# Hybrid decoder trunk: attention by pairs of tiles, and linear attention's scores of two chunks in one stretch

## The chip, the cores and the metric

The kernel runs on one core of a Trainium2 chip. The metric is the device time of one execution in microseconds (us); the time of a kernel is the median over its runs. An engine's busy time in the profile is the time in which it has at least one instruction in flight. The five engines are TensorE (PE, with its weight loads shown apart as PEld), VectorE (DVE), ScalarE (ACT), GpSimd (POOL) and SyncE (SP), which here issues most of the transfers.

## The reference

Two layers over a sequence of 1024 tokens with 1024 features, all in float32. A layer normalises the tokens, modulates them by a conditioning vector, projects them to the inputs of three groups of heads, gates the three outputs and projects them back:

```python
h = rms_norm(x, pre_gain) * (1.0 + scale) + shift
aq, ak, av, ag, rq, rk, rv, rg, gq, gk, gv, gg, ga = jnp.split(h @ w_in, IN_SPLITS, axis=-1)
a_out = sliding_window_attention(rot(aq), rot(ak), av, sinks) * silu(ag)      # 8 heads, 2 for keys and values
r_out = rms_norm(retention(rot(rq), rot(rk), rv)) * silu(rg)                  # 4 heads, chunks of 128
log_a = log_sigmoid(ga @ gla_gate_w + gla_gate_b) / 16
g_out = rms_norm(gated_linear_attention(gq, gk, gv, log_a), gain) * silu(gg)  # 4 heads, decay per key channel
x = x + gate * rms_norm(concat(a_out, r_out, g_out) @ w_out, post_gain)
```

Sliding-window attention looks back 128 tokens: a tile of 128 queries sees its own tile (keys up to the query) and the tile before it (keys after the query's place). A learned sink takes part in each softmax. Gated linear attention goes by chunks with a state that is carried from chunk to chunk:

```python
sc = einsum('bhid,bhijd,bhjd->bhij', qi, decay, ki)            # decay between i and j, per key channel
out = einsum('bhij,bhjv->bhiv', sc, vi) + einsum('bhid,bhdv->bhiv', qi * exp(b), state)
state = exp(b_last) * state + einsum('bhjd,bhjv->bhdv', ki * exp(b_last - b), vi)
```

## The kernel before

The 1024 tokens are eight tiles of 128 (t), in two halves of four (hf). A big projection is a sum of 24 matmuls over the full 128 by 128 array into one PSUM buffer of the pool `mm` (three buffers): each operand is split into a high and a low part, and three of the four products are summed. These matmuls are the stream that fills TensorE. Everything else on TensorE (scores, values, transposes, states) writes buffers of the pool `aux`, which has the other five of the eight PSUM banks, used in turn.

The order of TensorE's program is made by a small planner when the kernel is built. `clk` counts the estimated TensorE time of what is issued so far. Work beside the big projections is written as generators (`job`); a `yield` gives an estimated latency, from the table `L`, and may name a flag that must be set first; `pump`, called after every few matmuls of the stream, lets each job that is due issue its next step. So `L` doesn't delay anything on the chip: it says how far behind one step the next is placed in TensorE's program. Where a result is late on the chip, TensorE waits at that place, since its program is in order; so do the other engines, whose programs are in the order in which the jobs issue.

In a layer the order is gates, retention's inputs, linear attention's inputs, keys and values, queries of attention with their rotation (`attn_rot`, four times), attention's gates (`gate`, eight times), and the output projection (`y_half`). The small work is placed between these.

*Attention.* `attn_run` goes through the halves, the two groups of four heads (g) and the tiles, 16 (t, g) in a layer. For each, `attn_q` issues at once: the scores, 12 matmuls that use half of the array's rows each (64 features of a head; two of them run side by side), into two buffers of `aux`; the copy of the earlier tile's scores by ScalarE (`sprev`, L145) into the tile `smx`, and over it a masked copy of the own tile's scores by VectorE (L790); the maximum (L792), four exponentials on ScalarE (L795), a reciprocal (L798) and the normalisation on GpSimd (L799). The latency aq3 later it transposes the four heads' weights into one `aux` buffer (L176, `smx`), ScalarE copies them (`pf0`), GpSimd masks a second copy (L810). The latency aq4 later come the values: with the earlier tile's values `va` for all weights, and with the difference `vd` of own and earlier values for the masked ones: two matmuls each, in two passes (four in the trace), that use half of the array's columns. ScalarE copies the result (`aoc`), and a transfer puts it into `aoS` in DRAM, from where `gate` takes it when all four tiles of a half are there; the gated result goes to `mixS`, and the output projection loads it. Three `smx` tiles are in use in turn (SMB), and `load_mix` of the first two tiles waits for the flags ("s", l, 1, g) that attn_q sets when it issues the last scores of a half.

*Linear attention.* `gla_core` treats two chunk tiles (c) of 128 tokens as a pair p. For each c its scores are 28 matmuls of 32 columns, in two passes each (56 in the trace), that use a quarter of the array's rows, in four `aux` buffers, one for a head; ScalarE and VectorE bring them to `scz` (L985, L986). Then, the latencies gc3 and gc4 later, for each c: the part from the state (`stG`), the part from the scores, and, but for the last tile, the chunk's own addition to the state: four matmuls, in two passes, that use a quarter of the array's columns each (L1005), into a further `aux` buffer, which VectorE adds to `stC`.

Of the kernel before, what the change touches and what calls it, by code (L numbers as in the profile page):

```python
# [17 lines left out]
P = 128  # L18
# [71 lines left out]
def trunk(ctx: ExitStack, tc: tile.TileContext, ins, cst, out):  # L90
# [14 lines left out]
    def nm(s):  # L105
        uid[0] += 1
        return f"{s}_{uid[0]}"
# [75 lines left out]
    def job(gen):  # L183
        jobs.append([clk[0], None, gen])
# [579 lines left out]
    def attn_q(l, t, g, q):  # L764

        sm = gp.tile([P, 4, 129], F32, tag="smx", name=nm("smx"), bufs=SMB)
        V.tensor_copy(sm[:, :, 128], sink8[:, l, 4 * g:4 * g + 4])
        if t == 0:
            G.memset(sm[:, :, 0:128], -1e30)
        else:  # L770
            vd = gp.tile([P, P], F32, tag="vd", name=nm("vd"), bufs=3)
            G.tensor_tensor(vd, kv["v"][t], kv["v"][t - 1], ALU.subtract)
        pss = [aux(), aux()]
# [9 lines left out]
        if t % 4 == 3:  # L783
            flag(("s", l, t // 4, g))
        for r in range(2):
            pv = pss[r][:, 0:2 * n].rearrange("p (j c n) -> p j c n", j=2, n=P)
            sv = sm[:, r:4:2, 0:128]
            if t > 0:
                copy("sprev", sv, pv[:, :, 0, :])
            V.copy_predicated(sv, curmask.unsqueeze(1).to_broadcast((P, 2, P)), pv[:, :, n // P - 1, :])  # L790
        mx = small(4)
        V.tensor_reduce(mx, sm, AX.X, ALU.max, negate=True)  # L792
        sums = small(4)
        for h in range(4):
            A.activation(sm[:, h, :], sm[:, h, :], AF.Exp, bias=mx[:, h:h + 1],  # L795
                         accum_out=sums[:, h:h + 1])
        rs = small(4)
        V.reciprocal(rs, sums)  # L798
        eng("pn").tensor_tensor(sm[:, :, 0:128], sm[:, :, 0:128], rs.unsqueeze(2).to_broadcast((P, 4, P)), ALU.mult)  # L799
        yield lat("aq3", l)  # L800

        pp = aux()
        for h in range(4):
            transp(pp[:, h * P:(h + 1) * P], sm[:, h, 0:128], ident)
        pf = t2()
        copy("pf0", pf, pp)
        parts = [(kv["v"][max(t - 1, 0)], pf)]
        if t > 0:
            pr = t2()
            G.affine_select(h4(pr), h4(pf), [[0, 4], [1, P]], ALU.is_ge, 0.0, base=0, channel_multiplier=-1)  # L810
            parts.append((vd, pr))
        yield lat("aq4", l)
        po = aux()
        for q, (vt, pvv) in enumerate(parts):
            for r in range(2):
                mult(po[64 * r:64 * r + 64, 0:256].rearrange("p (j n) -> p j n", j=2), vt[:, 64 * r:64 * r + 64],
                     h4(pvv)[:, r:4:2, :], q == 0, q == len(parts) - 1, 0.215)
# [125 lines left out]
    def gla_core(l, p, qk, vs):  # L943
# [26 lines left out]
        A.activation(kbn, pt[:, 0:256], AF.Copy)  # L970
        for c in range(2):
            sp = [aux() for _ in range(4)]
            for s in range(1, 4):
                for h in range(4):
                    r = slice(32 * h, 32 * h + 32)
                    mult(sp[h][:, P + 32 * s:P + 32 * s + 32], kxz[r, s - 1, c],
                         q1[r, P * c + 32 * s:P * c + 32 * s + 32], True, True, 0.054)
            for s in range(4):
                for h in range(4):
                    r = slice(32 * h, 32 * h + 32)  # L980
                    dst = sp[h][:, 0:P].rearrange("p (b i) -> p b i", i=32)[:, :, 8 * s:8 * s + 8]
                    mult(dst, kds[s][r, P * c:P * c + P], cb32(ad[:, 0:256])[r, c, :, 8 * s:8 * s + 8],
                         True, True, 0.054)
            for h in range(4):
                A.activation(scz[:, c, h, 32:P], sp[h][:, P + 32:2 * P], AF.Copy)  # L985
                V.copy_predicated(scz[:, c, h, :], mask2, sp[h][:, 0:P])  # L986
            yield lat("gc3", l)
        yield lat("gc4", l)
        for c in range(2):
# [12 lines left out]
            if t < NT - 1:  # L1002
                pst = aux()
                for h in range(4):
# [314 lines left out]
L = {"tt1": 6.37, "tt2": 5.54, "tb1": 24.5, "tb2": 0.75, "pf3": 13.2, "pf1": 7.06, "pf2": 4.16, "mod1": 5.11, "mod2": 4.0, "mod3": 15.1, "mod4": 7.04, "mod5": 3.36, "mod6": 5.14, "pre1": 7.44, "kv1": 3.1, "kv2": 2.11, "aq1": 4.8, "aq7": 6.0, "ag1": 5.44, "aq2": 2.4, "aq6": 6.0, "aq3": 10.9, "aq4": 6.32, "aq5": 1.14, "hn1": 8.12, "hn2": 2.85, "gz1": 10.06, "gz2": 14.05, "gl1": 4.6, "gd3": 15.9, "gc1": 0.62, "gc2": 1.95, "gc3": 1.33, "gc4": 1.41, "gc6": 0.22, "gc5": 1.04, "rc1": 0.8, "rc2": 1.09, "rc3": 2.38, "rc4": 2.79, "fin1": 11.25, "lay1": 0.9, "mod2@1": 4.0, "mod3@1": 15.1, "mod5@1": 3.36, "mod6@1": 5.14, "pre1@1": 7.44, "kv1@1": 3.1, "kv2@1": 2.11, "aq1@1": 4.8, "aq7@1": 6.0, "ag1@1": 6.38, "aq2@1": 2.4, "aq6@1": 6.0, "aq3@1": 10.9, "aq4@1": 6.32, "aq5@1": 1.14, "hn1@1": 8.12, "hn2@1": 2.85, "gz1@1": 10.06, "gz2@1": 14.05, "gl1@1": 4.6, "gd3@1": 15.9, "gc1@1": 0.62, "gc2@1": 1.95, "gc3@1": 1.33, "gc4@1": 0.58, "gc6@1": 0.22, "gc5@1": 1.04, "rc1@1": 0.8, "rc2@1": 1.09, "rc3@1": 2.38, "rc4@1": 2.79, "fin1@1": 11.25, "lay1@1": 0.9}  # L1319
CHUNK = 7  # L1320
VDB = 8
FIN = 1
# [31 lines left out]
```

## Time and profile before

| | |
|---|---|
| time, median of 3 runs | 1030.42 us (1029.62 to 1031.78) |
| profiled execution: its time | 1029.6 us |
| its span | 1029.6 us |
| TensorE busy | 986.5 us, 96% |
| VectorE busy | 657.0 us, 64% |
| ScalarE busy | 385.2 us, 37% |
| GpSimd busy | 283.4 us, 28% |

A row of the timeline has the start, the length from the first start to the last end, the engine, line and operation, the tiles written and read (`out<-in`), the rows and columns of the array in use (64*128: half of the rows), the shape of the moving operand, and how many instructions the row merges. Matmuls overlap, so the length of a row reaches into the next; the time that a stretch takes is read from its start to the next row's start. In windows, a row has the stretch, its length, and the busy time of PE, PEld, DVE, ACT and POOL with the number of instructions; with a tile's name it has those engines alone that touch that tile. `arena` and `mx` hold weights and tokens of the big projections; but in rows with `kT,mx` the tile is the queries, and in `t,mx 32*128` linear attention's keys.

### The profile page before, as it was taken

How to read it: one execution, taken by the hardware profiler on the slowest of the kernel's cores; microseconds unless marked ns; L12 is line 12 of the kernel's file. 1: busy time of each engine (PE TensorE's matmuls, PEld its weight loads, DVE VectorE, ACT ScalarE, POOL GpSimd, SP SyncE). 2: the span in 40 equal slices, each digit the busy share in tenths (PEclk: the TensorE clock that was granted, in tenths of full speed). 3: DMA queues.
4: the chain of work that ended last, by engine and by line, in shares of the span. 5: the costliest groups of instructions: out<-in, count | busy, mean ns of one | idle time of the engine just before them, and what ended most of it. 6: DMA issues, size and time to landing. Idle time of an engine off the chain costs nothing.

```text
span 1029.6 us, 19500 instructions
## 1 busy us (share of the span) xinstructions
PE 986.5 (96%) x7185; PEld 837.6 (81%) x7185; DVE 657.0 (64%) x1597; ACT 385.2 (37%) x1098; POOL 283.4 (28%) x310
## 2 busy tenths in 40 slices
PE   5799999899999999999998999989999999999997
PEld 1588899888898777778888999988899877777886
DVE  3789856857657786664587395686676476653322
ACT  2465421323222565532353332123332266552111
POOL 2333101424231345421243120133233134532000
PEclk8899999999999999999998999999999999999999
DMA  9741613523326244687545151234132323445753
GB/s 324 270 133 52 180 50 103 147 84 101 99 78 195 76 147 129 213 264 224 189 146 162 42 164 53 79 111 124 34 107 73 113 82 98 149 123 184 226 190 137
DMA packets 124412, 140.47 MB, mean 136 GB/s; under 512 B 12718, under 2 KB 95640, under 8 KB 124316
## 3 DMA queue, kind: packets, MB, share of 16 engines
q1 hardware_dynamic: 116316, 127.50, 40.2%
q10 hardware_dynamic: 8000, 11.72, 3.2%
q8 instruction: 57, 0.93, 0.4%
q14 instruction: 39, 0.32, 0.1%
HBM read 102.48 MB, written 34.60 MB: 133 GB/s over the span
## 4 chain that ended last, share of the span: by engine, by line
PE 75%; DVE 11%; issue 3%; DMA 2%; POOL 2%; ACT 1%; SPq 0%; DVEq 0%; POOLq 0%; ACTq 0%
PE mm L161 58%; PE aux L161 13%; PE aux L176 4%; DVE arena L478 2%; DMA st<-in_w_mod_dram 1%; POOL sm L514 1%; DVE t L573 1%; DMA mx<-mixS 1%; DVE acc L361 1%; DVE t L420 0%; DVE t L544 0%; DVE t L844 0%; DVE t L1022 0%; DVE arena L147 0%; DVE t L924 0%
## 5 line engine op out<-in xcount | busy, mean ns | idle before, releaser
L161 PE MATMUL mm<-arena,arena 128*128 128x256 f32 (+2 forms) x1824 | 302.5, 320 | 6.0 <-DVE t L1092 3.8
L161 PE MATMUL mm<-arena 128*128 128x256 f32 (+2 forms) x1824 | 300.5, 318 | 7.2 <-ACT arena L577 3.0
L161 PEld LDWEIGHTS mm<-arena,arena 128*128 128x128 f32 x1824 | 256.0, 191 | 31.9 <-issue 4.0
L161 PEld LDWEIGHTS mm<-arena 128*128 128x128 f32 x1824 | 255.2, 191 | 31.3 <-issue 5.1
L161 PE MATMUL mm<-arena,mx 128*128 128x512 f32 (+1 forms) x816 | 184.9, 385 | 0.5 <-DMA mx<-mixS 0.5
L161 PEld LDWEIGHTS mm<-arena,mx 128*128 128x128 f32 x816 | 145.7, 188 | 34.7 <-issue 1.9
L514 POOL TENSOR_TENSOR sm<-sm,mhalf 128x1 f32<-128x1 f32 (+1 forms) x64 | 54.0, 845 | 329.2 <-DVE sm L513 318.5
L478 POOL TENSOR_TENSOR arena<-st,arena 128x512 fp32r<-128x512 f32 x66 | 95.7, 1459 | 104.6 <-ACT arena L145 75.3
L145 ACT ACTIVATE t<-aux 128x256 f32<-128x256 f32 (+2 forms) x112 | 52.5, 473 | 105.2 <-PE aux L176 62.0
L799 POOL TENSOR_TENSOR smx<-smx,sm 128x512 f32<-128x512 f32 x32 | 36.2, 1131 | 127.3 <-DVE sm L798 108.0
L478 DVE TENSOR_TENSOR arena<-st,arena 128x512 fp32r<-128x512 f32 x62 | 64.9, 1055 | 4.3 <-PE mm L161 2.7
L795 ACT ACTIVATE smx<-smx,sm 128x129 f32<-128x129 f32 x128 | 49.9, 392 | 34.5 <-DVE sm L792 29.1
L145 ACT ACTIVATE arena<-st 128x512 fp32r<-128x512 f32 x90 | 53.1, 625 | 21.3 <-PE mm L161 14.8
L361 DVE SCALAR_TENSOR_TENSOR acc<-st,c_act,acc 128x512 f32<-128x512 f32 x60 | 48.7, 812 | 17.3 <-DMA st<-in_w_mod_dram 17.0
L176 PE MATMUL aux<-c_ident,t 128*128 128x128 f32 x288 | 47.4, 282 | 7.7 <-DVE t L544 5.4
L1077 ACT ACTIVATE t<-mm 128x512 f32<-128x512 f32 x30 | 17.9, 596 | 97.0 <-PE mm L161 45.7
L1078 DVE TENSOR_TENSOR t<-mm,modg 128x512 f32<-128x512 f32 x30 | 20.7, 689 | 44.5 <-ACT t L1077 44.5
L1113 DVE SCALAR_TENSOR_TENSOR t<-t,sm,t 128x512 f32<-128x512 f32 x32 | 25.2, 813 | 35.9 <-DMA t<-xs 20.5
L176 PEld LDWEIGHTS aux<-c_ident,t 128*128 128x128 f32 x288 | 34.2, 143 | 13.9 <-DVE t L544 6.9
L161 PEld LDWEIGHTS aux<-t,mx 32*128 32x128 f32 (+1 forms) x896 | 40.1, 187 | 5.1 <-issue 3.2
L838 ACT ACTIVATE t<-aux 128x256 f32<-128x256 f32 x32 | 12.3, 383 | 82.0 <-PE aux L161 71.7
L161 PE MATMUL aux<-t,mx 32*128 32x32 f32 (+1 forms) x896 | 41.4, 272 | 0.7 <-DVE t L843 0.5
(191 smaller groups left out, 1252.0 us busy)
## 6 DMA issues: line engine op xcount, KB each, us to landing
st<-in_w_in_dram SPq DMA_DIRECT2D x96, 256.0 KB, 3.2
st<-in_w_mod_dram SPq DMA_DIRECT2D x64, 256.0 KB, 3.1
mx<-mixS SPq DMA_DIRECT2D x32, 512.0 KB, 5.4
mixS<-t SPq DMA_DIRECT2D x64, 128.0 KB, 2.0
st<-in_w_out_dram SPq DMA_DIRECT2D x32, 256.0 KB, 3.4
mixS<-t SPq DMA_DIRECT2D x32, 256.0 KB, 4.0
wm<-in_w_mod_dram SPq DMA_DIRECT2D x12, 512.0 KB, 6.6
t<-in_x_dram SPq DMA_DIRECT2D x24, 256.0 KB, 4.1
```

Of the source, the lines that this page charges most:

```text
L145: A.activation(dst, src, AF.Copy)
L161: T.matmul(dst, lhsT, rhs, start=start, stop=stop)
L176: T.transpose(dst, src, idn)
L361: V.scalar_tensor_tensor(acc, wt, c_act[:, k:k + 1], acc, ALU.mult, ALU.add)
L478: (G if first == 0 else eng(f"wlo{kc}")).tensor_tensor(wt[:, 1, 2 * kc:2 * kc + 2, 0:256], st, f(hi), ALU.subtract)
L514: G.tensor_tensor(r, r, mhalf[:, :w], ALU.pow)
L795: A.activation(sm[:, h, :], sm[:, h, :], AF.Exp, bias=mx[:, h:h + 1], accum_out=sums[:, h:h + 1])
L799: eng("pn").tensor_tensor(sm[:, :, 0:128], sm[:, :, 0:128], rs.unsqueeze(2).to_broadcast((P, 4, P)), ALU.mult)
L838: A.activation(sq, po, AF.Square)
L1077: A.activation(yg, pm, AF.Square, accum_out=ss[:, nh:nh + 1])
L1078: V.tensor_tensor(yg, pm, modg[l][:, 512 * nh:512 * nh + 512], ALU.mult)
L1113: V.scalar_tensor_tensor(xt[j], yg[j], r, xt[j], ALU.mult, ALU.add)
```

## The change

Attention is issued for pairs of tiles. `attn_run` issues, for a pair (t0, t0 + 1) of a half and group: the values of the pair two before it, where there is one (`attn_values`), then the scores of both tiles (`attn_scores`), with nothing in between. `attn_turn` then has the softmax of both tiles, the latency aq3, and the transposes of both. The values of two tiles go into the two halves of one `aux` buffer, with one copy and one transfer. Linear attention's scores of both chunks are issued in one stretch, into the same four buffers (a chunk has one half of each), followed at once by the state matmuls of both chunks into one buffer; the copies to `scz` treat both chunks at a time. There are more buffers: 13 instead of 10 of `t2`, 6 instead of 3 of `smx`, 6 instead of 3 of `vd`. The scratch for dynamic transfers is set to 1024 bytes of a partition. Where the diff is cut, the steps inside are those of before, for each tile or chunk. Many latencies in `L` have other values: in layer 0 aq1 4.8 to 6.95, aq3 10.9 to 10.84, aq4 6.32 to 8.15, aq5 1.14 to 2.88, gc3 1.33 to 1.88, gc4 1.41 to 1.31, tt2 5.54 to 6.45, rc2 1.09 to 1.47, ag1 5.44 to 6.32; in layer 1 gl1 4.6 to 12.56, aq6 6.0 to 9.44, gc3 1.33 to 2.91, gc4 0.58 to 0.91.

```diff
     def attn_run(l):
+        turned = []
         for hf in range(2):
             for g in range(2):
-                for t in range(4 * hf, 4 * hf + 4):
+                for t0 in (4 * hf, 4 * hf + 2):
                     yield (lat("aq7" if hf else "aq1", l), ("q", l, hf, g))
-                    yield (0.0, ("kT", l, t))
-                    job(attn_q(l, t, g, kv[(hf, g)]))
+                    for t in (t0, t0 + 1):
+                        yield (0.0, ("kT", l, t))
+                    if len(turned) == 2:
+                        yield (0.0, turned[0]["flag"])
+                        attn_values(l, turned.pop(0))
+                    held = dict(flag=("pf", l, t0, g), t0=t0, g=g)
+                    sms = [attn_scores(l, t, g, kv[(hf, g)], held) for t in (t0, t0 + 1)]
+                    if t0 % 4 == 2:
+                        flag(("s", l, hf, g))
+                    turned.append(held)
+                    job(attn_turn(l, held, sms))
+        for held in turned:
+            yield (0.0, held["flag"])
+            attn_values(l, held)
...
+    def attn_turn(l, held, sms):
+        for t, n, sm, pss in sms:
...
+        yield lat("aq3", l)
+        for t, n, sm, pss in sms:
...
+            held[("parts", t)] = parts
+        flag(held["flag"], lat("aq4", l))
+
+    def attn_values(l, held):
+        t0, g = held["t0"], held["g"]
         po = aux()
+        for i in range(2):
+            parts = held[("parts", t0 + i)]
+            for q, (vt, pvv) in enumerate(parts):
+                for r in range(2):
+                    mult(po[64 * r:64 * r + 64, 256 * i:256 * i + 256].rearrange("p (j n) -> p j n", j=2),
+                         vt[:, 64 * r:64 * r + 64], h4(pvv)[:, r:4:2, :], q == 0, q == len(parts) - 1, 0.215)
-        ao = t1()
-        copy("aoc", ao, po[:, 0:256])
-        dma("sao", aoS[t, :, 2 * g:2 * g + 2, :], ao.rearrange("p (k q) -> p k q", k=2))
-        flag(("ao", l, t, g), lat("aq5", l))
+        ao = t2()
+        copy("aoc", ao, po)
+        dma("sao", aoS[t0:t0 + 2, :, 2 * g:2 * g + 2, :].rearrange("t p k q -> p t (k q)"),
+            ao.rearrange("p (t n) -> p t n", t=2))
+        for i in range(2):
+            flag(("ao", l, t0 + i, g), lat("aq5", l))
...
     def gla_core(l, p, qk, vs):
+        sp = [aux() for _ in range(4)]
         for c in range(2):
-            sp = [aux() for _ in range(4)]
...
-            for h in range(4):
-                A.activation(scz[:, c, h, 32:P], sp[h][:, P + 32:2 * P], AF.Copy)
-                V.copy_predicated(scz[:, c, h, :], mask2, sp[h][:, 0:P])
-            yield lat("gc3", l)
+        pst = aux()
+        for c in range(2):
+            if 2 * p + c < NT - 1:
+                for h in range(4):
+                    mult(pst[32 * h:32 * h + 32, 64 * c:64 * c + 64], kbn[:, c * P + 32 * h:c * P + 32 * h + 32],
+                         vs[c][:, 64 * h:64 * h + 64], True, True, 0.03)
+        for h in range(4):
+            sv = sp[h].rearrange("p (c n) -> p c n", c=2)
+            A.activation(scz[:, :, h, 32:P], sv[:, :, P + 32:2 * P], AF.Copy)
+            V.copy_predicated(scz[:, :, h, :], mask2.unsqueeze(1).to_broadcast((P, 2, P)), sv[:, :, 0:P])
+        yield lat("gc3", l)
         yield lat("gc4", l)
...
-                pst = aux()
-                for h in range(4):
-                    mult(pst[32 * h:32 * h + 32, 0:64], kbn[:, c * P + 32 * h:c * P + 32 * h + 32],
-                         v[:, 64 * h:64 * h + 64], True, True, 0.03)
-                V.scalar_tensor_tensor(stC, stC, g[:, c, 24:25], pst[:, 0:64], ALU.mult, ALU.add)
+                V.scalar_tensor_tensor(stC, stC, g[:, c, 24:25], pst[:, 64 * c:64 * c + 64], ALU.mult, ALU.add)
...
-B2, B1, BS, BST, MMB, SMB = 10, 8, 11, 5, 3, 3
+B2, B1, BS, BST, MMB, SMB = 13, 8, 11, 5, 3, 6
+VDF = 6
...
-    nc = _bacc.Bacc("TRN2", target_bir_lowering=False, num_devices=1)
+    nc = _bacc.Bacc("TRN2", target_bir_lowering=False, num_devices=1,
+                     dynamic_dma_scratch_size=1024)
```

More of the change, by code (lines that the diff above doesn't have):

```diff
@@ L770, in attn_q @@
         else:
[L771 removed]
+            vd = gp.tile([P, P], F32, tag="vd", name=nm("vd"), bufs=VDF)
             G.tensor_tensor(vd, kv["v"][t], kv["v"][t - 1], ALU.subtract)
+            held[("vd", t)] = vd
+        held[("vp", t)] = kv["v"][max(t - 1, 0)]
         pss = [aux(), aux()]
@@ L793, in attn_q @@
-        sums = small(4)
-        for h in range(4):
[L795 to L802, printed above, removed]
-        for h in range(4):
-            transp(pp[:, h * P:(h + 1) * P], sm[:, h, 0:128], ident)
@@ L805, in attn_q @@
[L805 to L812, printed above, removed]
-        po = aux()
[L814 to L817, printed above, removed]
@@ L818, in attn_q @@
-        ao = t1()
-        copy("aoc", ao, po[:, 0:256])
-        dma("sao", aoS[t, :, 2 * g:2 * g + 2, :], ao.rearrange("p (k q) -> p k q", k=2))
-        flag(("ao", l, t, g), lat("aq5", l))
+        return t, n, sm, pss
+    def attn_turn(l, held, sms):
+        for t, n, sm, pss in sms:
+            for r in range(2):
+                pv = pss[r][:, 0:2 * n].rearrange("p (j c n) -> p j c n", j=2, n=P)
+                sv = sm[:, r:4:2, 0:128]
+                if t > 0:
+                    copy("sprev", sv, pv[:, :, 0, :])
+                V.copy_predicated(sv, curmask.unsqueeze(1).to_broadcast((P, 2, P)), pv[:, :, n // P - 1, :])
+            mx = small(4)
+            V.tensor_reduce(mx, sm, AX.X, ALU.max, negate=True)
+            sums = small(4)
+            for h in range(4):
+                A.activation(sm[:, h, :], sm[:, h, :], AF.Exp, bias=mx[:, h:h + 1],
+                             accum_out=sums[:, h:h + 1])
+            rs = small(4)
+            V.reciprocal(rs, sums)
+            eng("pn").tensor_tensor(sm[:, :, 0:128], sm[:, :, 0:128], rs.unsqueeze(2).to_broadcast((P, 4, P)), ALU.mult)
+        yield lat("aq3", l)
+        for t, n, sm, pss in sms:
+            pp = aux()
+            for h in range(4):
+                transp(pp[:, h * P:(h + 1) * P], sm[:, h, 0:128], ident)
+            pf = t2()
+            copy("pf0", pf, pp)
+            parts = [(held[("vp", t)], pf)]
+            if t > 0:
+                pr = t2()
+                G.affine_select(h4(pr), h4(pf), [[0, 4], [1, P]], ALU.is_ge, 0.0, base=0, channel_multiplier=-1)
+                parts.append((held[("vd", t)], pr))
+            held[("parts", t)] = parts
+        flag(held["flag"], lat("aq4", l))
```

22 lines of the change are left out of this document (7 added, 15 removed).

## Prediction, before the change was run

> **What bounds the kernel now.** I read the head of the page and the chain first, then the stages by windows, then the TensorE timeline row by row.
>
> ```profile
> span 1029.6 us, 19500 instructions
> PE 986.5 (96%) x7185; PEld 837.6 (81%) x7185; DVE 657.0 (64%) x1597; ACT 385.2 (37%) x1098; POOL 283.4 (28%) x310
> PE 75%; DVE 11%; issue 3%; DMA 2%; POOL 2%; ACT 1%; SPq 0%; DVEq 0%; POOLq 0%; ACTq 0%
> ```
>
> TensorE has work in flight in 96% of the span and carries 75% of the chain that ended last; 1029.6 − 986.5 = 43 us are gaps. Next, the two stages that the change edits, in both layers: linear attention (223 to 313, 716 to 806) and attention (335 to 448, 822 to 935). The columns are the busy us of each engine, then clock and DMA.
>
> ```profile
> 223.00:313.00 90.00, 87.93 (x1024) 81.42 (x1023) 62.15 (x205) 30.01 (x96) 27.82 (x41) 0.98 0.31 92
> 335.00:448.00 113.00, 113.00 (x684) 83.27 (x684) 81.09 (x156) 66.36 (x219) 49.71 (x52) 1.00 0.50 149
> 716.00:806.00 90.00, 89.43 (x1029) 81.98 (x1028) 59.66 (x199) 30.75 (x100) 28.48 (x37) 1.00 0.25 75
> 822.00:935.00 113.00, 113.00 (x677) 83.11 (x676) 74.44 (x140) 67.10 (x221) 47.78 (x51) 1.00 0.41 124
> ```
>
> In attention TensorE never stops, and in linear attention it stops for 2.1 and 0.6 us. So a gain can't come from a wait; it has to be TensorE time itself. The change leaves every matmul in place, so all that it can save is what a short stretch costs at its edges. The timeline has that price. The first row is a run of the big projection undisturbed (start, length, count, from the chain in order of time); the others are the timeline of TensorE in attention: kT is scores (S), va and vd are values (V), smx are transposes (T).
>
> ```profile
> 317.40 17.66 PE mm L161 x76
> ...
> 364.58 0.65 PE L161 MATMUL aux<-t,va 128*64 128x256 f32 x4
> ...
> 365.60 0.98 PE L161 MATMUL aux<-kT,mx 64*128 64x256 f32 x12
> 366.51 2.13 PE L161 MATMUL mm<-arena,arena 128*128 128x512 f32 x8
> ...
> 383.18 0.65 PE L161 MATMUL aux<-t,va 128*64 128x256 f32 x4
> 383.76 3.06 PE L161 MATMUL mm<-arena,arena 128*128 128x512 f32 x12
> ...
> 388.11 0.97 PE L161 MATMUL aux<-kT,mx 64*128 64x256 f32 x12
> 389.01 1.20 PE L161 MATMUL mm<-arena 128*128 128x512 f32 x4
> 390.14 0.65 PE L161 MATMUL aux<-t,va 128*64 128x256 f32 x4
> ...
> 391.15 3.06 PE L161 MATMUL mm<-arena 128*128 128x512 f32 x12
> ...
> 912.62 0.98 PE L161 MATMUL aux<-kT,mx 64*128 64x256 f32 x12
> 913.53 0.65 PE L161 MATMUL aux<-t,va 128*64 128x256 f32 x4
> ```
>
> Undisturbed, a matmul of the stream takes 17.66 / 76 = 0.232 us. The four between S (388.11) and V (390.14) take 390.14 − 389.01 = 1.13 us instead of 0.93: each return to the full-array stream between two stretches of half-array matmuls costs **0.20 us**. So S alone costs 0.90 + 0.20 = 1.10, V alone 390.14 to 391.15 and 0.20, 1.21. Joined, V and S take 364.58 to 366.51, 1.93 and one return: 2.13 against 2.31, so a join is worth about 0.20. V with one group of four (383.18 to 383.76) takes 0.58, with two 1.01: a further group adds 0.43 and no edge.
>
> **The change, part by part, on TensorE.**
>
> *Values of two tiles in a row.* Alone, four groups cost 0.58 + 3 × 0.43 + 0.20 = 2.07 instead of 2 × 1.21 = 2.42: 0.35 saved for each of 16 pairs, 5.6 us.
>
> *Scores of two tiles in a row.* No row shows two S in a row. The nearest is the time in which weights load for S, which a second S can't undercut by much:
>
> ```profile
> 335.00:463.00 128.00, 15.41 (x192) 12.26 (x192) 0.00 (x0) 0.00 (x0) 1.00 0.55 166
> ```
>
> 12.26 / 16 = 0.77 us of loading for one S, of the kT rows alone. I take 0.77 for the second S: 0.33 saved a pair, 5.3 us. Ends: only the return (0.20, 3.2 us) and half of S (0.55, 8.8 us).
>
> *Values beside scores.* attn_values and both attn_scores are issued with no yield between them, so they stand together by construction; 6 of 8 pairs in a layer have values two pairs back to join: 12 × 0.20 = 2.4 us. Before, 10 of the 64 stretches already stand so (the first at 365.60, the last at 913.53, counted along the timeline): 2.0 us are had already. Attention: 5.6 + 5.3 + 2.4 − 2.0 = **11.3 us**.
>
> *Linear attention.* Timeline again: `t,mx 32*128` are scores of a chunk, `stG` rows open its values, `t,t 128*32` are the state's.
>
> ```profile
> 229.88 1.54 PE L161 MATMUL aux<-t,mx 32*128 32x32 f32 x48
> 231.25 0.40 PE L161 MATMUL aux<-t 32*128 32x32 f32 x8
> 231.58 2.11 PE L161 MATMUL mm<-arena 128*128 128x512 f32 x8
> 233.62 1.54 PE L161 MATMUL aux<-t,mx 32*128 32x32 f32 x48
> ...
> 235.31 3.92 PE L161 MATMUL mm<-arena 128*128 128x256 f32 x31
> ...
> 242.44 1.00 PE L161 MATMUL aux<-t,mx 128*128 128x64 f32 x8
> ...
> 300.89 0.60 PE L161 MATMUL aux<-stG,t 128*128 128x256 f32 x2
> ...
> 302.25 0.32 PE L161 MATMUL aux<-t,t 128*32 128x64 f32 x8
> 302.50 0.33 PE L176 MATMUL aux<-c_ident,t 128*128 128x128 f32 x1
> 302.59 1.92 PE L161 MATMUL mm<-arena 128*128 128x256 f32 x14
> 304.34 0.59 PE L161 MATMUL aux<-stG,t 128*128 128x256 f32 x2
> ...
> 305.65 1.44 PE L161 MATMUL mm<-arena 128*128 128x256 f32 x10
> ```
>
> A chunk takes 235.31 − 233.62 = 1.69, and its return 2.04 − 8 × 0.232 = 0.18: 1.87. Inside, 48 take 231.25 − 229.88 = 1.37, 0.0285 each, so 56 more behind it add 1.60: 0.27 saved for each of 8 pairs, 2.2 us. A chunk's values with state matmuls take 302.59 − 300.89 = 1.70, without 305.65 − 304.34 = 1.31: the state costs 0.39, 14 times, 5.5 us. Behind the scores it costs its own 302.50 − 302.25 = 0.25, and for the second chunk 0.16 more, since about 0.09 of the 0.25, half a return, is the edge at its end: 8 × 0.41 = 3.3; 2.2 us saved. Ends for both edits together: 2.5 us (eight and six returns of 0.18) and 5.7 us (0.25 a pair for the states). The state matmuls now wait for kbn's copy on ScalarE earlier than before; the 112 score matmuls in front of them, 3.2 us, hide it. Linear attention: **4.4 us**.
>
> [...]
>
> **What lies beside it.** ScalarE copies of scores (64 of 96 columns become 32 of 192), masked VectorE copies (64 become 32 of double width), the values' copy and its store on SP's queue (32 become 16, twice as large), and more buffers: all off TensorE, 0. Values move behind the scores of the pair after next, and with them the store to aoS and what stands behind it on SP's queue, the gate's load and the store to mixS; the gate projections and the output projection of the other half keep TensorE full meanwhile (113.00 of 113.00 us), so 0 as well; without that cover new idle time would stand before the output projection (third rival). What gets tighter is the softmax of a pair: its second tile's copies queue behind the first tile's exponentials on ScalarE, and its masked copies behind the first's reciprocal on VectorE.
>
> ```profile
> L790 DVE COPY_PREDICATED smx<-c_curmask,aux x64: 431/447/466, 335.9 to 928.1; 128x256 f32<-128x256 int32 x64
> L792 DVE TENSOR_REDUCE sm<-smx x32: 673/691/693, 336.7 to 929.1; 128x4 f32<-128x516 f32 x32
> L795 ACT ACTIVATE smx<-smx,sm x128: 386/389/407, 337.5 to 930.9; 128x129 f32<-128x129 f32 x128
> L145 ACT ACTIVATE smx<-aux x56: 365/382/388, 342.5 to 926.8; 128x256 f32<-128x256 f32 x56
> ...
> 410.93 0.97 PE L161 MATMUL aux<-kT,mx 64*128 64x256 f32 x12
> 420.52 1.04 POOL L799 TENSOR_TENSOR smx<-smx,sm 128x512 f32<-128x512 f32 x1 [6.39 <-DVE smx L767]
> 424.84 0.60 PE L176 MATMUL aux<-c_ident,smx 128*128 128x128 f32 x4
> ```
>
> The second tile adds 0.38 + 2 × 0.45 + 0.69 + 4 × 0.39 = 3.5 us, less 0.77 because the first S ends earlier: 2.8 us. The tile with the least room of all 32 (scores at 410.93) is normalised at 421.56 and transposed at 424.84, 3.3 us later. aq3, the planner's distance from scores to transposes, stays 10.84 to 10.9. So it just fits in the worst place, but pairs now come in bursts, and VectorE is busy 81.09 of 113 us. I charge a third of 16 pairs with 0.5 us: **2.5 us**, an estimate; ends 0 and the rival below. In linear attention the values are far behind: scores end at 235.31 and their use is at 242.44. The five free PSUM buffers just hold one of values and four of scores; before, two chunks of linear attention took eight, now four.
>
> The planner's other numbers (gl1, tt2, rc2, ag1 and more) reorder the rest of TensorE's program. Their effect can't be read from this trace: I take 0, with ±5 us, of the 43 us of gaps. The smaller scratch makes room for the added buffers; what else it does no row shows, and it is in the same ±5.
>
> **Sum.** 1029.6 − 11.3 − 4.4 + 2.5 = 1016.4. The profiled execution's time is its span, 1029.6, with nothing around it, and 0.8 below the median of three (1030.42); I forecast 1016.5.
>
> **Rivals.**
>
> *Transposes wait for the second tile's softmax (slower).* Place: TensorE before the smx transposes. For: the two chains share ScalarE and VectorE in order, and there are only 0.5 us to spare in the worst place above. [...] Against: the transposes of no tile wait now. It decides from 15.7 / 16 = 1.0 us a pair; with 2.5 us, as if nothing of the 2.8 were covered, it gives 1029.6 − 15.7 + 40 = 1054; with 1.5 us, 1038.
>
> *Only returns are saved.* A second tile or chunk opens with an edge of its own, since it changes PSUM buffer. Then 32 × 0.20 + 12 × 0.20 − 2.0 + 8 × 0.18 + 6 × 0.20 = 9.4, less 2.5: 1022.7. For: no row shows two S in a row. Against: the second group of V changes operands and adds no edge.
>
> *Nothing arrives.* The freed time is waited away, by the reordered program or by VectorE, busy 62.15 of 90 us in linear attention: 1029 to 1031. Against: TensorE has projection matmuls between all stretches.
>
> **How the numbers follow.** Forecast 0.58 (1009 to 1020), only returns 0.21 (1020 to 1028), nothing 0.07, waiting transposes 0.14. The low end is the sum with the upper ends: 3.5 more for S, 1.3 more in linear attention and none of the 2.5 for softmax, 1016.4 − 7.3 = 1009. The range holds the first two cases, 1009 to 1028.5. A measurement tells 0.2%, 2.1 us, from no change: faster 0.79, same 0.07, slower 0.14.
>
> **What would show it.** Right: kT rows of x24, values of up to 16 beside them, 32*128 rows of both chunks without a projection row between, and the same matmul counts with less time from 335 to the output projection (about 5.6 us a layer) and in linear attention (2.2 us a layer). Wrong: idle time in front of the smx transposes (first rival), four-matmul gaps inside a stretch (second), new idle time before mm rows (third), or stalls elsewhere from the reordered program.

## The result and the profile after

The changed kernel took 1022.64 us (median of 7 runs, 1020.38 to 1024.44) beside 1030.42 us for the kernel before on the same chip (7 runs): a ratio of 0.9919, with a 95% interval from 0.9896 to 0.9941. The forecast was 1016.5 in a range of 1009 to 1028.5. The time lies in the range, some 6 us above the forecast. The parts behind it are less kind: two of them came out with the wrong sign or a wrong size, and cancelled.

The head of the page of the kernel after, and its chain of work by engine:

```profile
span 1020.9 us, 19368 instructions
PE 975.0 (96%) x7185; PEld 845.1 (83%) x7185; DVE 652.3 (64%) x1565; ACT 377.2 (37%) x1050; POOL 284.5 (28%) x310
PE 67%; DVE 13%; DMA 7%; issue 4%; ACT 3%; POOL 1%; SPq 1%; DVEq 0%; POOLq 0%; ACTq 0%
```

TensorE has the same 7185 matmuls and is busy for 11.5 us less. Both programs hold 4464 matmuls of the projection stream in the same order, so the two traces can be laid side by side at a given one of them (the 1040th, the 1500th and so on), which cuts the span into comparable stages:

| stage (by matmul of the stream) | before, us | after, us | difference | forecast |
|---|---|---|---|---|
| layer 0: up to linear attention (to 1040) | 223.1 | 223.4 | +0.2 | 0 |
| layer 0: linear attention (to 1500) | 104.4 | 108.2 | +3.8 | −2.2 |
| layer 0: attention (to 1960) | 151.0 | 148.5 | −2.6 | −4.4 |
| output projection, start of layer 1 (to 2560) | 114.1 | 109.7 | −4.4 | 0 |
| layer 1: projections, retention (to 3250) | 119.4 | 118.3 | −1.2 | 0 |
| layer 1: linear attention (to 3760) | 109.5 | 113.7 | +4.2 | −2.2 |
| layer 1: attention (to 4100) | 118.2 | 112.9 | −5.3 | −4.4 |
| layer 1: output projection | 89.9 | 86.4 | −3.5 | 0 |

(−4.4 in attention is −11.3 + 2.5, halved.) Attention gained 7.9 us, 0.9 less than forecast. Linear attention **lost 8.0** where 4.4 were to be gained. Stages that the diff hardly touches gained 8.8. Each has a cause of its own.

**The prices of the edges were right.** The timeline of TensorE after, a pair in layer 1's attention and a pair of chunks in layer 1's linear attention (start, length, name, count, idle time before it):

```profile
885.13 0.65 PE L161 MATMUL aux<-t,va 128*64 128x256 f32 x4
...
887.01 1.69 PE L161 MATMUL aux<-kT,mx 64*128 64x256 f32 x24
888.63 2.12 PE L161 MATMUL mm<-arena,arena 128*128 128x512 f32 x8
...
737.97 1.54 PE L161 MATMUL aux<-t,mx 32*128 32x32 f32 x48
...
739.56 1.52 PE L161 MATMUL aux<-t,mx 32*128 32x32 f32 x48
...
741.23 0.43 PE L161 MATMUL aux<-t,t 128*32 128x64 f32 x16
742.17 0.78 PE L176 MATMUL aux<-c_ident,t 128*128 128x128 f32 x4 [0.52 <-DVE mx L1018]
```

Values and scores of two tiles run from 885.13 to 888.63, 3.50 us; the terms gave 0.58 + 3 × 0.43 + 0.90 + 0.77 = 3.54. Scores and states of two chunks take 742.17 − 0.52 − 737.97 = 3.68 us; the terms gave 1.69 + 1.60 + 0.41 = 3.70.

**The clock in linear attention was not in the prediction.** Windows of the kernel after: the two stages that were shown of before (clock 0.98 and 1.00 there), then short stretches in them. The columns are busy us of PE, PEld, DVE, ACT and POOL, then the granted clock.

```profile
223.00:313.00 90.00, 86.89 (x991) 81.07 (x990) 59.65 (x177) 26.83 (x75) 32.12 (x43) 0.92 0.29 89
716.00:806.00 90.00, 88.46 (x1007) 82.83 (x1006) 56.27 (x170) 26.99 (x79) 30.13 (x40) 0.92 0.24 72
248.80:252.20 3.40, 1.43 (x22) 1.04 (x20) 3.34 (x10) 2.11 (x5) 0.83 (x1) 1.00 0.14 30
252.20:262.40 10.20, 10.20 (x134) 9.58 (x130) 4.45 (x10) 3.19 (x9) 1.89 (x3) 0.50 0.48 148
719.80:723.20 3.40, 3.40 (x105) 3.17 (x102) 0.69 (x3) 1.00 (x4) 1.30 (x3) 1.00 0.39 121
723.20:726.60 3.40, 3.40 (x16) 3.20 (x15) 3.40 (x11) 0.66 (x2) 1.29 (x3) 0.51 0.14 39
757.40:760.80 3.40, 3.40 (x114) 3.23 (x114) 3.40 (x13) 1.50 (x4) 0.90 (x2) 1.00 0.02 5
760.80:767.60 6.80, 6.53 (x54) 6.17 (x51) 4.00 (x14) 2.21 (x8) 1.99 (x5) 0.50 0.24 80
```

Five spells at half clock lie in linear attention, of 3.41, 6.83 or 10.24 us, 27.3 us together; before there was one of 3.41. The telling rows are 719.80 and 757.40: TensorE is busy for all of 3.40 us, with 105 and 114 matmuls, and the granted clock is 0.51 and 0.50 in the stretch behind. The score matmuls of two chunks, which use 32 rows of the array, take 2.4 us of the first window and 3.1 us of the second. The other three spells stand behind windows with waits: 2.0 us without work in the row 248.80, 0.5 and 0.6 us in the other two. At a granted clock of 0.50 I put the cost at no more than half of that time, an estimate: (27.3 − 3.4) / 2 = 12 us.

**Waits: not the softmax, but the PSUM buffers.** Rows of the waits of TensorE after (sum us, times, longest):

```profile
PE aux L176 <- DVE smx L807: 2.8, 3, 1.7
PE aux L176 <- DVE mx L1018: 2.6, 5, 0.6
PE mm L161 <- DVE t L1118: 1.1, 1, 1.1
...
410.64 0.63 PE L176 MATMUL aux<-c_ident,smx 128*128 128x128 f32 x4 [1.66 <-DVE smx L807]
```

The first row is attention; the second is linear attention, and the third the start of layer 1. L807 is the masked copy that empties the scores of the pair just computed. The transposes of the pair before need a second PSUM buffer, and where they follow at once on values and scores, that is the buffer of those scores. The softmax itself was in time everywhere: from its last product (the normalisation on GpSimd) to the transposes of the second tile there were 2.6 to 8.2 us.

### The profile page after: what moved, and what is told of

It reads as the page before. It is cut to its first block, busy times and chain, and to the rows that moved or that the text cites. A ratio compares the mean times of both kernels' runs of the same rounds, so it can differ in the third digit from the quotient of the medians.

```text
span 1020.9 us, 19368 instructions
## 1 busy us (share of the span) xinstructions
PE 975.0 (96%) x7185; PEld 845.1 (83%) x7185; DVE 652.3 (64%) x1565; ACT 377.2 (37%) x1050; POOL 284.5 (28%) x310
## 4 chain that ended last, share of the span: by engine, by line
PE 67%; DVE 13%; DMA 7%; issue 4%; ACT 3%; POOL 1%; SPq 1%; DVEq 0%; POOLq 0%; ACTq 0%
PE mm L161 52%; PE aux L161 11%; PE aux L176 4%; DMA st<-in_w_mod_dram 3%; DVE arena L478 1%; DVE acc L361 1%; DMA t<-t 1%; POOL sm L514 1%; DVE t L573 1%; ACT smx L812 1%; SPq L150 1%; DMA st<-in_w_out_dram 1%; DMA mx<-mixS 1%; DVE t L1050 1%; DVE smx L807 0%
## 5 line engine op out<-in xcount | busy, mean ns | idle before, releaser
L161 PE MATMUL mm<-arena,arena 128*128 128x256 f32 (+2 forms) x1824 | 294.3, 318 | 5.0 <-ACT sm L892 2.5
L161 PEld LDWEIGHTS mm<-arena 128*128 128x128 f32 x1824 | 258.5, 193 | 27.3 <-ACT arena L577 3.2
L161 PE MATMUL mm<-arena,mx 128*128 128x512 f32 (+1 forms) x816 | 180.2, 380 | 0.1
L145 ACT ACTIVATE t<-aux 128x512 f32<-128x512 f32 (+1 forms) x96 | 49.2, 522 | 114.3 <-PE aux L176 49.5
L816 POOL TENSOR_TENSOR smx<-smx,sm 128x512 f32<-128x512 f32 x32 | 35.2, 1100 | 112.9 <-DVE sm L815 109.1
L478 DVE TENSOR_TENSOR arena<-st,arena 128x512 fp32r<-128x512 f32 x62 | 60.5, 987 | 7.3 <-ACT arena L145 5.4
L145 ACT ACTIVATE arena<-st 128x512 fp32r<-128x512 f32 x90 | 52.3, 624 | 20.5 <-PE mm L161 10.9
L161 PEld LDWEIGHTS aux<-t,mx 32*128 32x128 f32 (+1 forms) x896 | 43.0, 200 | 4.5 <-DVE sm L273 1.4
L161 PE MATMUL aux<-t,mx 32*128 32x32 f32 (+1 forms) x896 | 44.2, 283 | 2.1 <-DVE sm L273 1.3
```

The costliest lines, as they stand in the source:

```text
L145: A.activation(dst, src, AF.Copy)
L161: T.matmul(dst, lhsT, rhs, start=start, stop=stop)
L478: (G if first == 0 else eng(f"wlo{kc}")).tensor_tensor(wt[:, 1, 2 * kc:2 * kc + 2, 0:256], st, f(hi), ALU.subtract)
```

## The experiments

**Attention alone.** The changed kernel with the old order of linear attention; its buffers and scratch are those of after.

```diff
  # of the changed kernel
- gla_core: 2 x 56 scores and 16 states in one stretch, gc* new
+ gla_core: 56 scores, projection matmuls, 56 scores; states with the values; gc* old
```

> The changed kernel with linear attention as it was (scores chunk by chunk, states beside the values, its four latencies as before). Clock theory: in the changed kernel the granted clock is at half for 10.2, 3.5, 3.4, 6.8 and 3.4 us in linear attention, 27 us in all against 3.4 us before, each spell after a stretch of 112 to 128 small matmuls; without those stretches the clock stays at 1.00 there, and the time falls by the 4.1 and 4.2 us that each layer's linear attention now loses, to 1014 to 1016 us. Rival (the stretches save what the prediction said, 4.4 us, and the loss has another cause, such as the new latencies): the time rises to about 1027 us.

1021.88 us (6 runs, 1018.31 to 1026.67), ratio 0.9921 [0.9898, 0.9945]: as fast as with the linear part, and not the 1014 to 1016 us of the theory. In the profiled executions (1016.6 us against 1020.9) two terms work against each other. There is no half-clock spell in linear attention, and its two stages take 211.5 us against 221.8 in the changed kernel, 10.3 less. But the start of layer 1 takes 115.5 us against 109.7, with a wait of 5.5 us that the account of the prediction comes back to.

**Linear attention alone.** The kernel before with only that part.

```diff
  # of the kernel before
- gla_core and gc* of before
+ gla_core and gc* of after
```

> The kernel before with the edit of linear attention alone (and its four latencies). Clock theory: half-clock spells appear in linear attention, and the time is 1033 to 1040 us. Prediction's theory (4.4 us saved): 1026 us. Neither: 1030.

1041.09 us (5 runs), ratio 1.0097 [1.0079, 1.0114]: by itself this part makes the kernel 10 us slower, a little more than the theory had, with seven half-clock spells of 30.7 us in the two linear attentions. In the profiled execution these two stages take 221.8 us against 213.9 before: what the edges save is less than what the clock takes. (Both runs change this part's four latencies with it; those were not tried apart.)

**More work between the chunks' scores.** The changed kernel with four full-array matmuls of 512 columns between the first and the second chunk's scores, added work that nobody reads (8 pairs × 4 × 0.232 = 7.4 us, and two more edges a pair).

```diff
+            if c:
+                pd = mm()
+                for _ in range(4):
+                    T.matmul(pd, h0[:, 0, 0, 0:P], both(h0, h1), start=True, stop=True)
             for s in range(1, 4):
```

> The changed kernel with four full-array matmuls of 512 columns, whose result nobody reads, between the scores of the two chunks of each pair: 8 x (4 x 0.232 + 0.20) = 9 us more work. Clock theory (a long stretch of small matmuls counts as too little activity): the half-clock spells in linear attention go, which gives back about 8 us, so 1022 to 1026 us at a higher mean clock. Rival (the clock falls because TensorE waits for buffers or copies near the stretch): the spells stay and the time is 1030 to 1033 us.

1028.81 us (11 runs), ratio 0.997 [0.9952, 0.9987] to before, between the two ranges. Three spells of 20.5 us remained, each behind a window with a wait in it, so this run did not separate the theories; the two behind fully busy windows were gone.

**The planner's numbers alone.** The kernel before with all new numbers but those of the edited functions (aq*, gc*).

> The kernel before with the new latencies of all steps but those of attention and of linear attention's chunks. If the reordered program is what takes 4.7 us off the step from layer 0 to layer 1 (540 to 555 us) in the changed kernel: 1024 to 1027 us, the 3.8 us wait for the last tile and the half-clock spell at 551 us gone. If those come from the attention edit: 1030 us.

1031.55 us (12 runs), ratio 1.0009 [0.9995, 1.0022]: nothing. The 8.8 us in stages that the diff does not touch are not from there.

**What the clock follows.** 704 matmuls of 512 columns in groups of 64, all without a wait, whose operands use a given number of rows and columns of the array.

```diff
+            for rows, cls in ((P, P), (32, 32), (P, P), (32, P), (P, P), (P, 32), (P, P),
+                              (64, 64), (P, P), (64, P), (P, P)):
+                for _ in range(64):
+                    T.matmul(pd[0:cls], h0[0:rows, 0, 0, 0:cls], both(h0[0:rows], h1[0:rows]),
+                             start=True, stop=True)
```

> The changed kernel with 704 added matmuls of 512 columns in linear attention of layer 0, all in one PSUM buffer that nobody reads, without any wait between them: 64 of the full array (128 x 128), 64 of 32 rows x 32 columns (1/16 of the array), 64 full, 64 of 32 x 128 (1/4), 64 full, 64 of 128 x 32 (1/4), 64 full, 64 of 64 x 64 (1/4), 64 full, 64 of 64 x 128 (1/2), 64 full. At full clock each group is about 13.7 us, four windows of 3.41 us. TensorE is 100% busy in all. Theory 'array share': clock 0.5 from the second window of the 1/16 group on (that group takes about 24 us), full in the 1/2 group (13.7 us), and the 1/4 groups (0.85 us of full array a window) lie at the border. Rival 'the clock follows idle time of TensorE': clock 1.0 in all groups, each 13.7 us. Rival 'the clock follows the number of rows alone, or of columns alone': 32 x 128 and 128 x 32 differ.

Windows inside the groups: full array, 32 × 32, 32 × 128, 128 × 32, 64 × 64, 64 × 128 (rows × columns).

```profile
250.00:262.00 12.00, 12.00 (x55) 9.93 (x54) 2.62 (x6) 1.56 (x4) 1.62 (x1) 1.00 0.39 111
270.00:283.00 13.00, 13.00 (x32) 5.05 (x31) 0.00 (x0) 0.00 (x0) 0.00 (x0) 0.50 0.00 0
310.00:324.00 14.00, 14.00 (x35) 10.64 (x34) 0.00 (x0) 0.00 (x0) 0.00 (x0) 0.50 0.00 0
345.00:358.00 13.00, 13.00 (x57) 6.10 (x56) 0.00 (x0) 0.00 (x0) 0.00 (x0) 1.00 0.00 0
376.00:386.00 10.00, 10.00 (x45) 5.75 (x44) 0.00 (x0) 0.00 (x0) 0.00 (x0) 1.00 0.00 0
404.00:416.00 12.00, 12.00 (x54) 9.71 (x53) 0.00 (x0) 0.00 (x0) 0.00 (x0) 1.00 0.00 0
```

TensorE is busy all the time in every row. Groups with 32 rows ran at a granted clock of 0.50 (0.40 to 0.41 us a matmul in these windows), also with all 128 columns (22.8 and 24.2 us a group); groups with 64 and 128 rows ran at 1.00 (0.22 to 0.23 us a matmul), also with few columns (14.6 to 14.9 us, where 13.7 were expected, and 16.2 and 16.4 for a full group behind one with 32 rows). 32 × 128, 128 × 32 and 64 × 64 use the same quarter of the array, so my theory of a share of the array falls, and that of idle time alone with it: in this run the clock followed the **rows** in use. 32 of 128 had 0.50 and 64 of 128 had 1.00; no number between was run.

The other traces fit this, with a border that is not sharp. Count a matmul's columns at 0.232 us for 512, times its share of the 128 rows, and add up what falls into each window of 3.41 us, the length of the shortest spell. In the other 13 profiles 3510 windows at full clock lie between 60 and 1000 us. Half clock follows on 41 of them, and in all 41 the sum is at most 1.31 us (27 of them under 1.0; of the 3469 others, 8 under 1.0, the least 0.72). Seven of the 41 have no idle time. Between 0.7 and 1.3 the sum does not decide.

**States early, chunk by chunk.** Attention alone as above, and each chunk's state matmuls right behind its scores; between two chunks the projection goes on.

```diff
+            if 2 * p + c < NT - 1:
+                for h in range(4):
+                    mult(sp[0][32 * h:32 * h + 32, 256:320], kbn[...], vs[c][...], True, True, 0.03)
+                A.activation(stp[:, 64 * c:64 * c + 64], sp[0][:, 256:320], AF.Copy)
```

> Base: the kernel with only the attention part changed (1021.9 us): linear attention's chunks are scored one by one with projection matmuls between, as before. Added: each chunk's four state matmuls stand right behind that chunk's scores and ScalarE copies their result out; nothing is joined over two chunks. Theory 'array share' (the clock is halved after a 3.41-us window in which the columns streamed, weighted by the share of the array they use, come to under about 0.7 to 1.0 us): a chunk's stretch of some 2 us always shares its window with full-array matmuls, so linear attention has no half-clock spell behind a window without idle time, and the saved returns (14 x 0.2 to 0.4 us) come through: 1017 to 1020 us, clock as in the base (0.985 to 0.989). Rival 'any work moved in front of the projection matmuls brings spells': spells as in the changed kernel, 1022 or more. Rival 'states cannot be saved there, because they wait for the copy of kbn': 1022 with a wait on ACT in front of the state matmuls.

**1016.72 us** (6 runs, 1014.97 to 1021.30), ratio 0.9865 [0.984, 0.9889]: the fastest kernel here. In the profiled executions it is 7.2 us ahead of the changed kernel (1013.7 against 1020.9), and the two linear attentions give 7.6 of that: 214.2 us against 221.8, with one half-clock spell, behind a window with 0.91 us of waits. So with the scores of the chunks apart most of the clock's price was gone (one spell against five), with no work added. Beside attention alone the gain is not from the states, though; linear attention's two stages took 211.5 us there. Waits of TensorE with states early:

```profile
PE aux L161 <- ACT t L995: 3.5, 4, 2.0
PE mm L161 <- DVE t L1117: 1.1, 1, 1.1
```

A chunk's stretch with states took 2.14 us instead of 1.89 and its values 1.33 instead of 1.72: 0.14 saved, 14 times, 2.0 us, and the state matmuls wait 3.5 us for ScalarE's copy of kbn (L995), the keys of the state's addition, as the rival said. What moved is the wait of the second row, at the start of layer 1, which was 5.5 us in the profile of attention alone: that stage takes 110.6 us against 115.5.

**Buffers and scratch alone.** The kernel before, its functions unchanged.

```diff
-B2, B1, BS, BST, MMB, SMB = 10, 8, 11, 5, 3, 3
+B2, B1, BS, BST, MMB, SMB = 13, 8, 11, 5, 3, 6        # and vd bufs 3 -> 6, scratch 1024
```

> The kernel before with only the added SBUF buffers (B2 13, SMB 6, six vd) and the smaller DMA scratch; the program's order of work is untouched except where it follows from a free buffer. My theory (the buffers only hold the pairs): no change, 1029 to 1031.5. Rival (the buffers or the scratch carry part of the gain by themselves): 1028 or less. Rival (the smaller scratch makes DMA issues wait): above 1033.

1022.99 us (7 runs, five from 1020.59 to 1025.05 and two at 1031), ratio 0.9937 [0.9904, 0.9969]. My theory was wrong: this edit carries a gain by itself, though not in every run. TensorE's program is the same, instruction for instruction, while the order of work on VectorE, ScalarE, GpSimd and SP's queue changes with them. The output projection of layer 1 shows something else as well: its full-array matmul of 512 columns takes 227 ns from start to start (median) instead of 234.

**Scratch alone, and scratch with the old addresses.** The first moves every SBUF tile down by 15,360 bytes a partition, the second fills that hole with an unused tile.

> The kernel before with only the smaller DMA scratch; buffers as before. All SBUF tiles lie 15,360 bytes per partition lower. The kernel with scratch and buffers measured 1023.0 us against 1030.8, with the same order of TensorE's program, and in its output projection of layer 1 a full-array matmul of 512 columns took 227 ns instead of 234. Theory 'scratch or placement': this kernel is as fast, 1021 to 1025 us, and has the 227 ns. Theory 'buffers': no change, 1029 to 1032 us, 234 ns.

> As the kernel with only the smaller scratch, and an unused tile of 15,360 bytes per partition in front, which puts every tile back to its address of before. Theory 'placement' (where the tiles lie in SBUF sets the 7 ns): as before, 1029 to 1032 us and 234 ns. Theory 'the size of the scratch itself': as the kernel with only the scratch. Theory 'buffers': no change in both.

1031.75 us, ratio 0.9999 [0.9979, 1.0019], and 1030.69, ratio 1.0002 [0.9981, 1.0023], both with 234 ns. The scratch shows no effect, within 0.2%; it makes room.

**32 bytes.** An unused tile of 32 bytes a partition ahead of the second weight buffer: in the kernel before, in the kernel with buffers alone, in the changed kernel.

```diff
+    ap.tile([P, 8], F32, name="pad")
     arenas.append(ap.tile([P, 4 * SLOT], F32R, name="arena1"))
```

> The kernel before with one edit: an unused tile of 32 bytes per partition ahead of the second weight buffer (arena1), which then begins at a multiple of 64 bytes (163648), as it does by chance in every kernel here with the added buffers; before, and in the kernels with the smaller scratch alone, it begins 32 bytes beside one. Nothing else changes, no buffer is added. Theory 'alignment': the full-array matmul in layer 1's output projection takes 227 ns instead of 234, the start and the output projection shorten, and the kernel is as fast as the one with the buffers, 1021 to 1026 us. Theory 'buffers': no change, 1029 to 1032 us and 234 ns.

> The kernel before with the smaller scratch and all added buffers (1023.0 us), and the same 32 unused bytes, which here put the second weight buffer 32 bytes beside a multiple of 64. Theory 'alignment': back to 1029 to 1032 us and 234 ns. Theory 'buffers': still 1021 to 1025 us. In between: both.

> The changed kernel (1022.6 us) with the same 32 unused bytes, which put its second weight buffer 32 bytes beside a multiple of 64, as before the change. Theory 'alignment': what alignment gave (about 5 to 8 us) is lost, 1027 to 1031 us, and what is left against before is the gain of the edits on TensorE (some 17 us at full clock) less what the half-clock spells in linear attention take. Theory 'the gain is that of the edits': 1021 to 1025 us.

| kernel | arena1 at byte | matmul, ns | us | ratio to before |
|---|---|---|---|---|
| before | 163616 | 234 | 1031.28 | |
| before + 32 bytes | 163648 | 234 | 1030.99 | 1.0007 [0.9992, 1.0021] |
| buffers | 162176 | 227 | 1022.99 | 0.9937 [0.9904, 0.9969] |
| buffers + 32 bytes | 162208 | 234 | 1028.03 | 0.9969 [0.9956, 0.9983] |
| after | 162176 | 227 | 1022.64 | 0.9919 [0.9896, 0.9941] |
| after + 32 bytes | 162208 | 234 | 1024.99 | 0.9941 [0.992, 0.9962] |

(Each ratio is to the kernel before on the same chip; the first row's time is that of the runs with 32 bytes. The bytes are worked out from the 163648 of the expectation and the sizes of the tiles in front; no trace shows them.) The windows 950 to 970 of buffers alone and of the same with 32 bytes count it, 90 matmuls in 20 us against 87:

```profile
950.00:970.00 20.00, 20.00 (x90) 16.57 (x89) 7.53 (x14) 2.75 (x8) 0.77 (x2) 1.00 0.74 242
...
950.00:970.00 20.00, 20.00 (x87) 16.05 (x87) 8.51 (x17) 2.58 (x8) 1.23 (x2) 1.00 0.84 264
```

Every engine's program in these two has the same order, so the 7 ns come from where the weights lie. In the changed kernel layer 1's output projection takes 88.6 us with the 32 bytes and 86.4 without. My rule for it, a multiple of 64 bytes, falls with the second row of the table. The fast places of this buffer (also 163200, in states early, where the 816 matmuls on arena and mx are busy for 180.3 us beside 180.2 in the changed kernel and 184.9 before) are multiples of 128, the slow ones are not; that was seen, and not tested. Buffers with the 32 bytes lie between the two theories, still clear of no change; the changed kernel with them lies at the upper end of the second theory's range. The intervals of the last two rows overlap, and so do those of the two above: that the 32 bytes change the time of the whole run is likely by the medians, not shown.

## Why the prediction came out as it did

*Edges in attention: right.* The working by rows (0.20 a return, 0.77 for a second S, 0.43 a further group) met the joined stretch within 0.04 us; of its scores, 887.01 to 888.63, 1.62 − 0.90 = 0.72 us are the second S. Layer 1's attention, where one wait of 0.40 us is left, gained 5.3 us against 5.65 forecast before softmax; layer 0's gained 2.6, with 3.0 us of waits that before did not have. With the buffers alone the two stages take 269.5 us, as before the change (269.3), so this gain is the edit's. The rival of returns only, in which a second S keeps its edge (0.90 instead of 0.77), falls with the same rows.

*Softmax, 2.5 us: right in size by luck, wrong in place.* TensorE waits 2.8 us before the smx transposes, for a PSUM buffer and not for the softmax. "The five free PSUM buffers just hold one of values and four of scores" had the count, and missed that the transposes come next and need two more.

*Linear attention, 4.4 us: wrong sign.* The working of the step holds at full clock: subtract half of the half-clock time of each trace, the estimate of above, and the two stages go from 212.1 us to 208.2, 3.9 us less. What it left out is the clock, which was in no row of before that I read as a price: one spell of 3.41 us, at 271.15, behind one chunk's scores and a wait of 0.61 us. One stretch has 3.3 us in 32-row matmuls, nearly as long as the shortest spell, 3.41 us. The five spells after begin at 252.20, 279.51, 723.24, 760.79 and 784.68, whole multiples of 3.41 us apart, and windows of that grid without idle time brought them too: TensorE is busy for all of 3.40 us in those of 719.80 and 757.40. Why the spells keep to that grid no run shows.

*The rest, 0 with ±5: wrong.* Its stages gave 8.8 us. The planner's numbers gave nothing of it. The buffers, which I put off TensorE at 0, reorder the other engines and move the weights. Where the time went at the start of layer 1 is a row of VectorE. The timeline of before, VectorE and GpSimd (here by start), then the first matmul behind; then the same place with buffers alone:

```profile
544.99 1.30 POOL L478 TENSOR_TENSOR arena<-st,arena 128x512 fp32r<-128x512 f32 x1 [2.69 <-ACT arena L145]
545.38 2.94 DVE L147 CAST arena<-st 128x512 fp32r<-128x512 f32 x1
546.23 1.81 POOL L660 MEMSET mx<- 128x2048 f32 x1
548.00 1.44 POOL L581 TENSOR_TENSOR arena<-t,arena 128x512 fp32r<-128x512 f32 x1
548.24 3.42 DVE L478 TENSOR_TENSOR arena<-st,arena 128x512 fp32r<-128x512 f32 x2
549.40 1.71 POOL L478 TENSOR_TENSOR arena<-st,arena 128x512 fp32r<-128x512 f32 x1
551.66 0.41 DVE L1092 TENSOR_TENSOR t<-mm,modg 128x256 f32<-128x256 f32 x1
552.12 8.09 PE L161 MATMUL mm<-arena,arena 128*128 128x272 f32 x42 [3.77 <-DVE t L1092]
...
541.13 1.29 POOL L478 TENSOR_TENSOR arena<-st,arena 128x512 fp32r<-128x512 f32 x1 [2.68 <-ACT arena L145]
541.52 1.19 DVE L147 CAST arena<-st 128x512 fp32r<-128x512 f32 x1
542.37 2.09 POOL L660 MEMSET mx<- 128x2048 f32 x1
542.63 1.28 DVE L478 TENSOR_TENSOR arena<-st,arena 128x512 fp32r<-128x512 f32 x2
543.90 0.41 DVE L1092 TENSOR_TENSOR t<-mm,modg 128x256 f32<-128x256 f32 x1
544.37 3.27 PE L161 MATMUL mm<-arena,arena 128*128 128x272 f32 x24 [0.61 <-DVE t L1092]
```

The cast takes 2.94 us in the one and 1.19 in the other, the two subtractions 3.42 and 1.28. In the first each ends only behind two instructions of GpSimd that follow each other without a gap (the cast at 548.32 and GpSimd's fill at 548.04; the subtractions at 551.66 and GpSimd's at 551.11); in the second VectorE comes in between, and GpSimd's fill takes 2.09 us instead of 1.81. The multiplication behind (L1092) empties the PSUM buffer that the next projection waits for, 3.77 us against 0.61, and in before a half-clock spell of 6.83 us begins at 551.04, within the wait. The rows show neither why nor what decides: in both, the cast starts 0.39 us behind GpSimd's first instruction and 0.85 ahead of its second, and only in one does it come in between. With the 32 bytes added to the buffers, and the same order on every engine, the wait was 3.85 us again, and in attention alone 5.5. So this term is luck as much as buffers.

Of the 3.5 us in layer 1's output projection, 2.2 go with the place of the weights (88.6 us with the 32 bytes, 86.4 without). The other 1.3 stay open.

*Nothing arrives, and waiting transposes,* did not happen; the sign came out as forecast, and the time in its range, but by luck. The two edits were to give 13.2 us after softmax and gave nothing together (7.9 gained, 8.0 lost). The 7.8 us come from stages that were put at 0, and buffers alone would have given as much. With the 32 bytes in both, the changed kernel is 3.0 us ahead of buffers alone (1024.99 against 1028.03), but that isn't the edits' worth: the intervals of their ratios overlap, and in the profiled executions linear attention loses 9.6 us, attention gains 6.5 and the start of layer 1 gains 3.9. Only states early, which has attention's edit without the long stretches, has an interval (0.984 to 0.9889) clear below that of buffers alone (0.9904 to 0.9969).

## What to carry to other kernels

Price an edge by the stretches that the trace already holds, but price the clock too: before matmuls of few rows are put together, count how much of a 3.41-us window they fill (2.4 us were enough here); on TensorE, two short stretches with full-row work between them can be better than one long (linear attention's two stages took 211.5 us so, against 221.8). Split a change by its parts and give buffers and placement a run of their own: a change can be carried by what was thought to be only its means, and a forecast can come true for the wrong reasons. And where transposes or copies take PSUM buffers in turn, count those of the next step as well.

## What the hardware showed that was not expected

- The granted clock followed the rows in use, in one run with TensorE never idle in these groups: 0.50 for 32 × 32 and 32 × 128, 1.00 for 64 × 64 and 128 × 32.
- A full-array matmul of 512 columns took 227 or 234 ns, 3%, with 32 bytes between the two places of its weights (buffers alone, without and with the 32 bytes); the rule behind it stays open.
- VectorE's cast of 512 columns took 0.41 us with no large instruction of GpSimd beside it (the row below, of the kernel after) and 2.94 behind two of them (above).

```profile
539.74 0.41 DVE L147 CAST arena<-st 128x512 fp32r<-128x512 f32 x1
```
